# Six instead of four of eleven up-projection blocks by Strassen's method, with two more load buffers and one shared tile, in a two-layer encoder trunk on one core

## The chip, the core and the metric

The kernel runs on one core of one Trainium2 chip. The metric is device time in microseconds (us) of one execution, and lower is better. The time before is 1370.86 us, the median of three runs (1370.63 to 1371.48).

## What is computed

Two encoder layers run on 512 tokens of width 1024. Each layer has a token mixer (retention and neighbourhood attention in the first, a state-space scan in the second) and then a gated channel mixer, each between two RMS norms. The change touches the channel mixer alone, which runs once in each layer:

```python
def conv_geglu_ffn(hn, w_up, conv_w, conv_b, w_down):
    u = depthwise_conv_centered(hn @ w_up, conv_w, conv_b)   # 512x1024 @ 1024x5632
    gate, val = jnp.split(u, 2, axis=-1)                     # 2816 gate, 2816 value columns
    return (jax.nn.gelu(gate, approximate=True) * val) @ w_down
```

All data are 32-bit floats.

## The kernel before, in words

**Products of 32-bit numbers.** Each operand is kept as two tiles of the type fp32r, a high part and what is left (the names end in `h`/`hi` and `l`/`lo`). `split` makes the pair: ScalarE casts the source to the high part (`whi`, L107), and VectorE subtracts that from the source (`wlo`, L108). `mm3` multiplies with three matmuls: high by high (L116), low by high (L117) and high by low (L118). In the up projection the weights are the stationary operand and come first, so the second matmul of a product already needs the low part of its weights (the rows name them "out<-moving,stationary").

**The up projection** (`ffn`). The 2816 gate and 2816 value columns are cut into 22 tiles of 128 features, index `f`. Tiles 0 and 1 are computed together, in halves of the tokens. From then on tiles go in pairs, which makes eleven blocks with the first. A *plain* pair loads four weight units of 128x1024 (gate and value of both tiles, 512 KB each), splits each one, and makes 96 matmuls of 512 columns. A *Strassen* pair (`up_strassen`, for `f` in `UP`) treats the two tiles as a 2x2 block product over halves of the 1024 inputs and halves of the 512 tokens, with gate and value as the two rows of blocks, and needs seven block products instead of eight. Each of the seven products, `i` = 0 to 6, is 24 matmuls of 256 columns. Its weights are one of the four loaded quarters (`q[11]`, `q[12]`, `q[21]`, `q[22]`) or a sum of quarters that VectorE adds (`add`, L447), then a split of 128x1024. The combined activations come from `combos`, once in a layer. Results go from PSUM to the tiles `G` and `V` by ScalarE copies (L489) and VectorE additions (L447). The low half of `V` and the two halves of `G` each collect two products.

**Behind each tile** `tail` makes the convolution and the gate. For each of gate and value there is one ScalarE pass (L507) and two VectorE passes (L508, L509), then the activation (L514), and the product into `H` (L516).

**Buffers.** Weights of the up and down projections land in a pool of three load buffers (`wst`). A Strassen block holds three quarters there and the fourth, with one sum, in the pool `gain`. The pools `whi` and `wlo` have four buffers each. Thus the split for a product can be made when the product four before it has left TensorE. `G` and `V` alternate between two pairs of tiles.

**The down projection** (`down_strassen`) is a Strassen product too. Four of its weight combinations are built in HBM by DMAs that GpSimd issues (`sums`, L274), 32 of them in a layer. `chore(n)` starts the next n of them behind a named product of the up projection.

**Order.** The program is written in the order above, and a scheduler places the instructions on each engine's queue. Splits and weight sums stand in a section of higher priority (60). Each engine then works through its queue in that fixed order.

Of the kernel before, what the change touches and what calls it, by code (L numbers as in the profile page):

```python
# [8 lines left out]
F32 = mybir.dt.float32  # L9
R32 = mybir.dt.float32r  # L10
# [3 lines left out]
ALU = mybir.AluOpType  # L14
# [3 lines left out]
P = 128  # L18
# [7 lines left out]
HK = NF // 2  # L26
HW = S // 2
# [247 lines left out]
    return out  # L275


def down_strassen(E, big, pool, w, ts, H, first, g_post, done):

    nc, tc = E.nc, E.tc
    lower, upper = slice(0, HW), slice(HW, S)
    A11, A21 = H[:, :HK, upper], H[:, :HK, lower]
    A12, A22 = H[:, HK:, upper], H[:, HK:, lower]
    k0 = [0]

    def stage(i, u, cols):
        st = pool.tile([P, 1024], F32, name="wx", tag="k3") if k0[0] % 4 == 3 else E.wst.tile([P, 1024], F32, name="wst")
        k0[0] += 1  # L290
        nc.sync.dma_start(st[:, :cols], quarters(*i)[u])
        return st[:, :cols]

    def weights(i, u, extra=None):
        cols = 1024 if u < HK // 2 else 512
        st = stage(i, u, cols)
        if extra is None:
            hi, lo = E.whi.tile([P, 1024], R32, name="whi"), E.wlo.tile([P, 1024], R32, name="wlo")
        else:
            hi, lo = extra[:, :1024], extra[:, 1024:]  # L300
        with tc.high_priority(150):
            E.split(hi[:, :cols], lo[:, :cols], st)
        return [(hi[:, c:c + 512], lo[:, c:c + 512]) for c in range(0, cols, 512)]

    a, bb = ([E.mm.tile([P, 512], F32, name="mm") for _ in range(2)] for _ in range(2))
    d = []

    def raw(i):
        tt, stt = nc.vector.tensor_tensor, nc.vector.scalar_tensor_tensor
        if i == 1:  # L310
            s3 = big.tile([P, HK, HW], F32, name="s3")
            tt(s3, A11, A21, op=ALU.subtract)
            return s3
        if i == 2:
            tt(A21, A22, A21, op=ALU.subtract)
            stt(A11, A11, -1.0, A21, op0=ALU.mult, op1=ALU.subtract)
            return A11
        if i == 6:
            stt(A11, A12, -1.0, A11, op0=ALU.mult, op1=ALU.subtract)
            return A11  # L320
        return {3: A22, 4: A21, 5: A12}[i]

    def prepare(i):
        if i % 2:
            hi, lo = (E.res.tile([P, HK, HW], R32, name="a" + n, tag=n) for n in ("xh", "xl"))
        else:
            hi, lo = (big.tile([P, HK, HW], R32, name="a" + n, tag=n) for n in ("b1h", "b1l"))
        src = raw(i)
        for c in (slice(0, 5), slice(5, HK)):
            E.split(hi[:, c], lo[:, c], src[:, c])  # L330
        return hi, lo

    seq = ((w, 0), a), ((ts, 1), bb), ((ts, 2), a), ((ts, 3), bb), ((ts, 0), a), ((w, 2), d), ((w, 3), a)
    kept = {}
    st = {}
    op, nxt = first, None
    started = []
    for i, (src, bank) in enumerate(seq):
# [12 lines left out]
        if last:
            ex = {4: big.tile([P, 2048], R32, name="x1", tag="s3"), 5: big.tile([P, 2048], R32, name="x2", tag="e2")}
            ws = [weights(src, u, ex.get(u)) for u in range(HK // 2 + 1)]
            for t in range(2):
                for u, x in enumerate(ws):
                    if (t, u) == (0, 1):
                        E.operands()
                    if u == 1:
                        E.finish(f"t{t}", st, done)
                    mms(t, x, u)  # L360
                E.post_half(st, 2 + t, 1, bank[t], g_post, sign=-1.0)
                E.finish(f"x{2 + t} s{2 + t}", st, done)
# [24 lines left out]

UP = (6, 10, 14, 18)


def combos(E, pool, raw):


    tt, stt = E.nc.vector.tensor_tensor, E.nc.vector.scalar_tensor_tensor
    f32 = lambda ap: ap.bitcast(F32)
    lower, upper = slice(0, HW), slice(HW, S)
    out = {}
    block = lambda k, c: (slice(None), slice(4 * k, 4 * k + 4), c)

    def whole(i, k, c):  # L400
        b = block(k, c)
        tt(raw[:, i], f32(E.xh[b]), f32(E.xl[b]), op=ALU.add)
        return raw[:, i]

    def parts(n, tag, src):
        x = pool.tile([P, 2, 4, HW], R32, name="x" + n, tag=tag)
        E.split(x[:, 0], x[:, 1], src)
        out[n] = x[:, 0], x[:, 1]

    for n, k, c in (("A11", 0, upper), ("A12", 1, upper), ("A22", 1, lower)):  # L410
        out[n] = E.xh[block(k, c)], E.xl[block(k, c)]
    r1, a21 = whole(0, 1, lower), whole(1, 0, lower)
    tt(r1, r1, a21, op=ALU.subtract)
    parts("R1", "b1h", r1)
    yield out
    s2 = whole(2, 0, upper)
    tt(a21, s2, a21, op=ALU.subtract)
    parts("S3", "b1l", a21)
    yield out
    stt(s2, s2, -1.0, r1, op0=ALU.mult, op1=ALU.subtract)  # L420
    parts("S2", "s3", s2)
    yield out
    s4 = whole(3, 1, upper)
    stt(s4, s4, -1.0, s2, op0=ALU.mult, op1=ALU.subtract)
    parts("S4", "e2", s4)
    yield out


def up_strassen(E, w_up, f, X, G, V):

    nc, tc = E.nc, E.tc
    low, high = slice(0, HW), slice(HW, S)

    def load(pool, name, s, h):
        st = pool.tile([P, 1024], F32, name=name)
        nc.sync.dma_start(st.rearrange("p (f c) -> p f c", f=2),
                          w_up[s, f:f + 2, :, h * 512:h * 512 + 512].rearrange("f p c -> p f c"))
        return st  # L440
# [7 lines left out]
    q = {}  # L448

    def weights(i):  # L450
        with tc.high_priority(60):
            if i == 0:
                q[11] = load(E.wst, "wst", 0, 0)
                return parts(q[11])
            if i == 1:
                q[12], q[22] = load(E.wst, "wst", 1, 0), load(E.wst, "wst", 1, 1)
# [16 lines left out]
    for i, (n, bank) in enumerate(order):  # L473
# [15 lines left out]
                nc.scalar.copy(o, r)  # L489
        if i == 4:  # L490
            add(V[:, :, low], t, V[:, :, low])
        if i in (2, 5):
            E.chore(2)


def ffn(E, w_up, cw, w_down, ts, g_post_row, done, w1=None):
# [3 lines left out]
    with ExitStack() as ctx:  # L500
# [17 lines left out]
        def extra(tags):  # L518
# [4 lines left out]
        u0, u1, st = w1 or (E.wunit(w_up[0, 0]), E.wunit(w_up[1, 0]), None)  # L523

        behind = E.turned[1][1] if w1 else None
        w0 = [[u0, u1], [E.wunit(w_up[0, 1], extra(("b1h", "b1l")), st, behind=behind),
                         E.wunit(w_up[1, 1], extra(("e2",)), behind=behind)]]
        cwt = cp.tile([P, 2, NF, 4], F32, name="cwt")
        nc.sync.dma_start(cwt, cw)
        cwn = cp.tile([P, NF, 3], F32, name="cwn")  # L530
# [11 lines left out]
        for f in range(2, NF):  # L542
            if f in UP or f - 1 in UP:
                if f in UP:
                    G, V = (cp.tile([P, 2, S], F32, name=n, tag=t) for n, t in
                            ((("G", "k0"), ("V", "k1")) if UP.index(f) % 2 else (("G", "k2"), ("V", "k3"))))
                    up_strassen(E, w_up, f, X, G, V)
# [12 lines left out]
            if f < UP[0]:  # L560
                X = next(make)
            if f == NF - 2:
                first = [hp.tile([P, HK, HW], R32, name="a" + n, tag=n) for n in ("b1h", "b1l")]
                for k in range(0, HK, 4):
                    c = slice(k, min(k + 4, HK))
                    E.split(first[0][:, c], first[1][:, c], H[:, c, HW:])
        g_post = E.bcast(g_post_row)
        down_strassen(E, hp, cp, w_down, ts, H, first, g_post, done)


def log1p_exp_neg(E, alloc, z):
# [884 lines left out]
```

## Time and profile before

| what | us |
|---|---|
| median of three runs | 1370.86 |
| the profiled execution | 1372.97 |
| its span (first to last instruction) | 1371.2 |
| TensorE busy with matmuls | 1344.3 |
| VectorE busy | 1088.5 |
| ScalarE busy | 815.2 |
| one Strassen pair on TensorE (from `f` = 6) | 20.15 |
| one plain pair on TensorE (from `f` = 8) | 21.79 |

The profiled execution is one run, 2.11 us above the median, and 1.77 us of it lie outside its span. "PE" is TensorE, "PEld" its weight loads, "DVE" VectorE, "ACT" ScalarE, "POOL" GpSimd, and "SP" the engine that issues most DMAs. A row of the timeline gives the start, the duration, the engine and line, what is written and read, and in brackets the idle time before it and what ended that. A row of the stretches gives the stretch, its length, and the busy time of each engine in it with the number of its instructions. Instructions of VectorE overlap a little at their ends, so the distance from start to start is what one costs in an unbroken row.

### The profile page before, as it was taken

The numbers are of one execution on the slowest core, as the hardware profiler recorded it, in microseconds if no ns is written. First come the engines' busy times: TensorE is split into PE (matmuls) and PEld (weight loads), VectorE is DVE, ScalarE is ACT, GpSimd is POOL, SyncE is SP. The second block draws the span as 40 slices with busy tenths as digits, with TensorE's granted clock in tenths as the row PEclk, the third lists the DMA queues.
The fourth block names the chain that finished last, engine by engine and source line by source line (L and its number), as shares of the span: only waits on it lengthen the run. The fifth ranks groups of instructions, "written<-read, shape, count | busy, mean of one in ns | idle before, by whom it ended". The sixth has DMA issues, their size and how long they took to land.

```text
span 1371.2 us, 19491 instructions
## 1 busy us (share of the span) xinstructions
PE 1344.3 (98%) x7352; PEld 1136.2 (83%) x7352; DVE 1088.5 (79%) x1524; ACT 815.2 (59%) x1345; POOL 111.5 (8%) x130
## 2 busy tenths in 40 slices
PE   7999999999999999999999999999999999999997
PEld 6877777798999888888778788787878899998886
DVE  7368878696768889697878876898789877888876
ACT  5356667453554566664878778477555455556563
POOL 1001110100111100020000110000010001110000
PEclk9999999999999999999999999999999999999999
DMA  7443232126779946654566455174433678994654
GB/s 298 144 138 99 89 100 93 49 93 218 256 210 233 250 147 193 197 201 128 142 180 194 119 178 179 48 204 110 147 128 127 224 249 214 234 242 131 196 179 145
DMA packets 73471, 229.90 MB, mean 168 GB/s; under 512 B 8352, under 2 KB 9120, under 8 KB 72864
## 3 DMA queue, kind: packets, MB, share of 16 engines
q1 hardware_dynamic: 58320, 167.30, 37.3%
q0 software_dynamic: 7168, 46.14, 13.4%
q10 hardware_dynamic: 7888, 15.21, 4.1%
q8 instruction: 58, 0.95, 0.3%
q14 instruction: 37, 0.30, 0.1%
HBM read 221.01 MB, written 51.64 MB: 199 GB/s over the span
## 4 chain that ended last, share of the span: by engine, by line
PE 83%; ACT 6%; DVE 5%; DMA 3%; issue 2%; POOL 1%; DVEq 0%; SPq 0%; POOLq 0%; ACTq 0%
PE mm L116 23%; PE mm L118 23%; PE mm L117 23%; PE pu L118 2%; PE pu L117 2%; PE pu L116 2%; PE pi L1122 1%; PE st L1071 1%; ACT pb L1101 1%; DMA pb<-pd 1%; PE py L1142 1%; ACT whi L107 1%; DVE wlo L108 1%; DMA wst<-in_c_fm 1%; PE pt L173 1%
## 5 line engine op out<-in xcount | busy, mean ns | idle before, releaser
L116 PE MATMUL mm<-xh,whi 128*128 128x512 f32 (+1 forms) x1024 | 382.5, 374 | 0.8 <-ACT z L1041 0.4
L118 PE MATMUL mm<-xl,whi 128*128 128x512 f32 (+1 forms) x1024 | 381.6, 373 | 1.0 <-DVE xl L108 0.5
L117 PE MATMUL mm<-xh,wlo 128*128 128x512 f32 (+1 forms) x1024 | 381.3, 373 | 1.0 <-DVE wlo L108 1.0
L108 DVE TENSOR_TENSOR wlo<-wst,whi 128x1024 fp32r<-128x1024 f32 (+1 forms) x232 | 280.9, 1216 | 89.9 <-ACT whi L107 88.3
L107 ACT CAST whi<-wst 128x1024 fp32r<-128x1024 f32 (+1 forms) x232 | 239.2, 1035 | 145.8 <-PE mm L117 63.5
L116 PEld LDWEIGHTS mm<-xh,whi 128*128 128x128 f32 x1024 | 192.6, 188 | 35.9 <-issue 2.3
L118 PEld LDWEIGHTS mm<-xl,whi 128*128 128x128 f32 x1024 | 192.2, 188 | 35.6 <-issue 1.3
L117 PEld LDWEIGHTS mm<-xh,wlo 128*128 128x128 f32 x1024 | 192.6, 188 | 34.2 <-DVE wlo L108 1.4
L1101 ACT ACTIVATE pb<-pb,tok 128x128 f32<-128x128 f32 x256 | 80.8, 393 | 9.3 <-DMA pb<-pd 7.9
L507 ACT ACTIVATE cv<-mm,cwt 128x512 f32<-128x512 f32 x56 | 43.5, 777 | 68.8 <-PE mm L118 68.7
L118 PE MATMUL mm<-wlo,ab1h 128*128 128x512 f32 x164 | 64.0, 390 | 0.4 <-DVE wlo L108 0.4
L116 PE MATMUL mm<-whi,ab1h 128*128 128x512 f32 x164 | 64.0, 390 | 0.0
L117 PE MATMUL mm<-whi,ab1l 128*128 128x512 f32 x164 | 63.8, 389 | 0.0
L508 DVE SCALAR_TENSOR_TENSOR cv<-mm,cwt,cv 128x511 f32<-128x511 f32 x56 | 41.7, 745 | 22.2 <-ACT cv L507 22.2
L514 ACT ACTIVATE cv<-cv 128x512 f32<-128x512 f32 x44 | 27.8, 632 | 42.8 <-DVE cv L509 42.8
L1035 DVE SCALAR_TENSOR_TENSOR xf<-mm,cwt,xf 128x511 f32<-128x511 f32 (+1 forms) x64 | 47.6, 745 | 6.2 <-ACT xf L1032 5.8
L274 POOL DMA_DIRECT2D ts<-in_f_down x48 | 30.0, 668 | 261.7 <-PE mm L118 227.7
L509 DVE SCALAR_TENSOR_TENSOR cv<-mm,cwt,cv 128x511 f32<-128x511 f32 x56 | 41.8, 746 | 0.9
L116 PE MATMUL mm<-whi,yh 128*128 128x512 f32 x104 | 40.8, 394 | 1.5 <-DVE xf L1035 1.5
L1154 POOL TENSOR_TENSOR sq<-sq 128x512 f32<-128x512 f32 x11 | 16.7, 1516 | 309.1 <-ACT sq L1148 244.6
L117 PE MATMUL mm<-whi,yl 128*128 128x512 f32 x104 | 41.1, 395 | 0.0
L116 PE MATMUL mm<-whi,xh 128*128 128x512 f32 x104 | 40.7, 398 | 0.0
(359 smaller groups left out, 2919.7 us busy)
## 6 DMA issues: line engine op xcount, KB each, us to landing
wst<-in_f_up SPq DMA_DIRECT2D x80, 512.0 KB
ts<-in_f_down POOLq DMA_DIRECT2D x48, 704.0 KB, 6.2
wst<-in_c_fm SPq DMA_DIRECT2D x40, 512.0 KB
wst<-ts SPq DMA_DIRECT2D x32, 512.0 KB
pb<-pd ACTq DMA_DIRECT2D x29, 512.0 KB
wst<-in_f_down SPq DMA_DIRECT2D x24, 512.0 KB
ts<-ts POOLq DMA_DIRECT2D x16, 704.0 KB, 9.9
wst<-in_ab_fm SPq DMA_DIRECT2D x20, 512.0 KB
```

Source lines behind the costliest of these rows:

```text
L107: first = self.nc.scalar.copy(hi, src)
L108: second = self.nc.vector.tensor_tensor(lo, src, hi.bitcast(F32), op=ALU.subtract)
L116: mm(out, lh, rh, start=first, stop=False)
L117: mm(out, ll, rh, start=False, stop=False)
L118: self.product = mm(out, lh, rl, start=False, stop=last)
L274: out.append(lambda i=i, src=src, j=j, c=c, kw=kw: gp.dma_start(part(ts, i, c), part(src, j, c), **kw))
L507: nc.scalar.activation(o, ps, AF.Identity, scale=w(1), bias=w(3))
L508: nc.vector.scalar_tensor_tensor(o[:, 1:], ps[:, :S - 1], w(0), o[:, 1:], op0=ALU.mult, op1=ALU.add)
L509: nc.vector.scalar_tensor_tensor(o[:, :S - 1], ps[:, 1:], w(2), o[:, :S - 1], op0=ALU.mult, op1=ALU.add)
L514: nc.scalar.activation(g, g, AF.Gelu_apprx_tanh)
L1035: nc.vector.scalar_tensor_tensor(r[:, a], ps[:, b], wc(j), r[:, a], op0=ALU.mult, op1=ALU.add)
L1101: nc.scalar.activation(pb[:, dr, c], pb[:, dr, c], AF.Identity, scale=1.0 - 2 * dr, bias=tok[:, 0, c, dr * H + h:dr * H + h + 1])
```

## The change

1. `UP` becomes (6, 8, 10, 14, 16, 18). The pairs at 8 and 16 are now Strassen pairs, in both layers. Before, each Strassen pair stood between plain pairs; now there are two groups of three in a row.
2. The first quarter of a Strassen block, `q[11]`, is loaded into a buffer of its own (name `wu`), alternating between two tiles `e0` and `e1`, and no longer into `wst`.
3. The four split combined activations share one tile, `xc`, instead of four tags. It has the tag `big`, which the operands of the down projection take over afterwards (`big[:, 0]`, `big[:, 1]`, and `big[:, 2]` for weights).
4. The first operand that the down projection prepares, a difference, is made in three pieces through `e0` and `e1` instead of one piece in a tile of its own.
5. A Strassen block starts one chore behind each of the products 1, 3 and 5, instead of two behind 2 and 5.

```diff
-        if i == 1:
-            s3 = big.tile([P, HK, HW], F32, name="s3")
-            tt(s3, A11, A21, op=ALU.subtract)
-            return s3
...
-            hi, lo = (big.tile([P, HK, HW], R32, name="a" + n, tag=n) for n in ("b1h", "b1l"))
+            hi, lo = big[:, 0], big[:, 1]
+        if i == 1:
+            for n, c in enumerate((slice(0, 4), slice(4, 8), slice(8, HK))):
+                s3 = hp.tile([P, 4, HW], F32, name="s3", tag=f"e{n % 2}")[:, :c.stop - c.start]
+                nc.vector.tensor_tensor(s3, A11[:, c], A21[:, c], op=ALU.subtract)
+                E.split(hi[:, c], lo[:, c], s3)
+            return hi, lo
...
-UP = (6, 10, 14, 18)
+UP = (6, 8, 10, 14, 16, 18)
...
-    def parts(n, tag, src):
-        x = pool.tile([P, 2, 4, HW], R32, name="x" + n, tag=tag)
-        E.split(x[:, 0], x[:, 1], src)
-        out[n] = x[:, 0], x[:, 1]
+    x = pool.tile([P, 4, 2, 4, HW], R32, name="xc", tag="big")
+
+    def parts(n, i, src):
+        E.split(x[:, i, 0], x[:, i, 1], src)
+        out[n] = x[:, i, 0], x[:, i, 1]
...
-                q[11] = load(E.wst, "wst", 0, 0)
+                q[11] = load(pool, "wu", 0, 0, f"e{UP.index(f) % 2}")
...
-        if i in (2, 5):
-            E.chore(2)
+        if i in (1, 3, 5):
+            E.chore()
...
-                first = [hp.tile([P, HK, HW], R32, name="a" + n, tag=n) for n in ("b1h", "b1l")]
+                big = hp.tile([P, 3, HK, HW], R32, name="big")
                 for k in range(0, HK, 4):
                     c = slice(k, min(k + 4, HK))
-                    E.split(first[0][:, c], first[1][:, c], H[:, c, HW:])
+                    E.split(big[:, 0, c], big[:, 1, c], H[:, c, HW:])
```

In the changed kernel every line of `up_strassen`, `ffn` and what follows stands four lines further down (L447 becomes L451, L489 L493, L507 to L516 L511 to L520); `split` and `mm3` keep their lines.

**VectorE's queue behind the last split of a Strassen block.** Before, at the block of `f` = 10, in the first layer. The first row is the split for product 6. The `wlo<-wst` rows after it are units of the plain pair that follows, L447 are additions into `G` and `V`, and L508 begins the tail.

```order
L108 TENSOR_TENSOR wlo<-wst,whi 128x1024
L447 TENSOR_TENSOR G<-pu,G 128x256 x2
L108 TENSOR_TENSOR wlo<-wst,whi 128x1024
L447 TENSOR_TENSOR V<-w_3745,V 128x2x256
L108 TENSOR_TENSOR wlo<-wst,whi 128x1024
L447 TENSOR_TENSOR G<-pu,G 128x256 x2
L108 TENSOR_TENSOR wlo<-wst,whi 128x1024
L508 SCALAR_TENSOR_TENSOR cv_3811<-G,cwt,cv_3811 128x511
```

Now, at the block of `f` = 6, which another Strassen block follows. The first row is again the split for product 6. The row `wlo<-wu` is the split for product 0 of the next block, and the L451 rows of 128x1024 are its weight sums.

```order
L108 TENSOR_TENSOR wlo<-wst,whi 128x1024
L451 TENSOR_TENSOR G<-pu,G 128x256 x2
L108 TENSOR_TENSOR wlo<-wu,whi 128x1024
L451 TENSOR_TENSOR wu<-wu,wst 128x1024
L451 TENSOR_TENSOR V<-w_3337,V 128x2x256
L451 TENSOR_TENSOR wst<-wst 128x1024
L451 TENSOR_TENSOR G<-pu,G 128x256
L451 TENSOR_TENSOR gain<-wu,wst 128x1024
L451 TENSOR_TENSOR G<-pu,G 128x256
L108 TENSOR_TENSOR wlo<-wst,whi 128x1024
L512 SCALAR_TENSOR_TENSOR cv_3402<-G,cwt,cv_3402 128x511
L108 TENSOR_TENSOR wlo<-gain,whi 128x1024
```

The three weight sums of the next block have moved between the additions into `G` and `V`, ahead of the tail. The same queue goes on with the tail of the first block up to the split for product 3 of the second (the last row here; the row `gain<-gain` is the sum that it reads):

```order
L513 SCALAR_TENSOR_TENSOR cv_3402<-G,cwt,cv_3402 128x511
L512 SCALAR_TENSOR_TENSOR cv_3407<-V,cwn,cv_3407 128x511
L512 SCALAR_TENSOR_TENSOR cv_3412<-G,cwt,cv_3412 128x511
L513 SCALAR_TENSOR_TENSOR cv_3407<-V,cwn,cv_3407 128x511
L513 SCALAR_TENSOR_TENSOR cv_3412<-G,cwt,cv_3412 128x511
L520 TENSOR_TENSOR H<-cv_3402,cv_3407 128x512
L512 SCALAR_TENSOR_TENSOR cv_3417<-V,cwn,cv_3417 128x511
L451 TENSOR_TENSOR gain<-gain 128x1024
L513 SCALAR_TENSOR_TENSOR cv_3417<-V,cwn,cv_3417 128x511
L520 TENSOR_TENSOR H<-cv_3412,cv_3417 128x512
L108 TENSOR_TENSOR wlo<-gain,whi 128x1024
```

The whole tail of one Strassen block now stands ahead of product 3's split of the next.

**VectorE's queue where the down projection's difference is made.** Before, inside the last Strassen block (`f` = 18), in one piece:

```order
L108 TENSOR_TENSOR wlo<-gain,whi 128x1024
L312 TENSOR_TENSOR s_4833<-H 128x2816
L108 TENSOR_TENSOR wlo<-wst,whi 128x1024
```

Now the first piece stands in the block of `f` = 16, behind the split for product 0 of the block of `f` = 18 (`wlo<-wu`), a second piece one block later, and the third in the down projection:

```order
L451 TENSOR_TENSOR G<-pu,G 128x256 x2
L108 TENSOR_TENSOR wlo<-wu,whi 128x1024
L327 TENSOR_TENSOR s_5047<-H 128x1024
L451 TENSOR_TENSOR V<-w_4509,V 128x2x256
L451 TENSOR_TENSOR wu<-wu,wst 128x1024
```

The first piece has moved ahead of the last Strassen block's weight sums. GpSimd's queue has the same rows as before, and the second layer's channel mixer has the same order as the first's.

More of the change, by code (lines that the diff above doesn't have):

```diff
@@ L275, in sums, with down_strassen @@
     return out
-def down_strassen(E, big, pool, w, ts, H, first, g_post, done):
+def down_strassen(E, hp, pool, w, ts, H, big, g_post, done):
     nc, tc = E.nc, E.tc
@@ L299, in weights @@
         else:
-            hi, lo = extra[:, :1024], extra[:, 1024:]
+            hi, lo = extra
         with tc.high_priority(150):
@@ L335, in down_strassen @@
     st = {}
-    op, nxt = first, None
+    op, nxt = (big[:, 0], big[:, 1]), None
     started = []
@@ L351, in down_strassen @@
         if last:
-            ex = {4: big.tile([P, 2048], R32, name="x1", tag="s3"), 5: big.tile([P, 2048], R32, name="x2", tag="e2")}
+            x = big[:, 2].rearrange("p k c -> p (k c)")
+            ex = {4: (x[:, :1024], x[:, 1024:2048]), 5: [hp.tile([P, 1024], R32, name="x2", tag=n) for n in ("e0", "e1")]}
             ws = [weights(src, u, ex.get(u)) for u in range(HK // 2 + 1)]
@@ L413, in combos @@
     tt(r1, r1, a21, op=ALU.subtract)
-    parts("R1", "b1h", r1)
+    parts("R1", 0, r1)
     yield out
@@ L417, in combos @@
     tt(a21, s2, a21, op=ALU.subtract)
-    parts("S3", "b1l", a21)
+    parts("S3", 1, a21)
     yield out
     stt(s2, s2, -1.0, r1, op0=ALU.mult, op1=ALU.subtract)
-    parts("S2", "s3", s2)
+    parts("S2", 2, s2)
     yield out
@@ L424, in combos, with up_strassen, load @@
     stt(s4, s4, -1.0, s2, op0=ALU.mult, op1=ALU.subtract)
-    parts("S4", "e2", s4)
+    parts("S4", 3, s4)
     yield out
-def up_strassen(E, w_up, f, X, G, V):
+def up_strassen(E, pool, w_up, f, X, G, V):
     nc, tc = E.nc, E.tc
     low, high = slice(0, HW), slice(HW, S)
-    def load(pool, name, s, h):
-        st = pool.tile([P, 1024], F32, name=name)
+    def load(pool, name, s, h, tag=None):
+        st = pool.tile([P, 1024], F32, name=name, tag=tag or name)
         nc.sync.dma_start(st.rearrange("p (f c) -> p f c", f=2),
@@ L525, in ffn @@
         behind = E.turned[1][1] if w1 else None
-        w0 = [[u0, u1], [E.wunit(w_up[0, 1], extra(("b1h", "b1l")), st, behind=behind),
-                         E.wunit(w_up[1, 1], extra(("e2",)), behind=behind)]]
+        w0 = [[u0, u1], [E.wunit(w_up[0, 1], extra(("big",)), st, behind=behind),
+                         E.wunit(w_up[1, 1], extra(("e0", "e1")), behind=behind)]]
         cwt = cp.tile([P, 2, NF, 4], F32, name="cwt")
@@ L546, in ffn @@
                             ((("G", "k0"), ("V", "k1")) if UP.index(f) % 2 else (("G", "k2"), ("V", "k3"))))
-                    up_strassen(E, w_up, f, X, G, V)
+                    up_strassen(E, hp, w_up, f, X, G, V)
                     for j in range(2):
@@ L562, in ffn @@
             if f == NF - 2:
-                first = [hp.tile([P, HK, HW], R32, name="a" + n, tag=n) for n in ("b1h", "b1l")]
+                big = hp.tile([P, 3, HK, HW], R32, name="big")
                 for k in range(0, HK, 4):
                     c = slice(k, min(k + 4, HK))
-                    E.split(first[0][:, c], first[1][:, c], H[:, c, HW:])
+                    E.split(big[:, 0, c], big[:, 1, c], H[:, c, HW:])
         g_post = E.bcast(g_post_row)
-        down_strassen(E, hp, cp, w_down, ts, H, first, g_post, done)
+        down_strassen(E, hp, cp, w_down, ts, H, big, g_post, done)
 def log1p_exp_neg(E, alloc, z):
```

## The prediction

> **What bounds the kernel now.** I read the page's totals and its chain first, then stretches of the first layer's up projection, then the timelines of TensorE and VectorE in them.
>
> ```profile
> PE 1344.3 (98%) x7352; PEld 1136.2 (83%) x7352; DVE 1088.5 (79%) x1524; ACT 815.2 (59%) x1345; POOL 111.5 (8%) x130
> ...
> PE 83%; ACT 6%; DVE 5%; DMA 3%; issue 2%; POOL 1%; DVEq 0%; SPq 0%; POOLq 0%; ACTq 0%
> ...
> L118 PE MATMUL mm<-wlo,ab1h 128*128 128x512 f32 x164 | 64.0, 390 | 0.4 <-DVE wlo L108 0.4
> ```
>
> TensorE is 98% busy and carries 83% of the chain that ended last. So fewer matmul columns pay directly, as long as nothing else comes late. In the down projection (last row) TensorE idled 0.4 us in all. The pairs `f` = 6 to 19, Strassen and plain in turn:
>
> ```profile
> core 0: us, PE busy (x) PEld busy (x) DVE busy (x) ACT busy (x) POOL busy (x), PEclk, DMA share, GB/s
> 342.70:362.85 20.15, 20.15 (x169) 20.14 (x168) 12.75 (x16) 11.75 (x19) 2.91 (x6) 1.00 0.69 243
> 362.85:384.64 21.79, 21.79 (x98) 18.03 (x97) 20.58 (x25) 10.87 (x15) 0.97 (x2) 1.00 0.64 235
> 384.64:404.79 20.15, 20.15 (x169) 20.14 (x168) 11.50 (x14) 9.54 (x16) 3.68 (x5) 1.00 0.77 206
> 404.79:426.58 21.79, 21.79 (x98) 18.04 (x97) 20.66 (x26) 12.85 (x18) 2.61 (x3) 1.00 1.05 264
> ...
> sum 145.97, PE 145.97 PEld 134.67 DVE 116.17 ACT 81.53 POOL 18.85; mean PE 20.85 PEld 19.24 DVE 16.60 ACT 11.65 POOL 2.69
> ```
>
> TensorE has no gap at all here. VectorE is busy only 12 to 13 us in a Strassen pair but over 20 in the plain pair behind it: it does the Strassen pair's tail and the next one's weight sums in the plain pair. That is the cover which the change takes away. That the ends of the stretches are the pairs' ends shows in TensorE's timeline (columns of a matmul change from 512 to 256 and back):
>
> ```profile
> 342.48 0.39 PE L118 MATMUL mm<-xl,whi 128*128 128x512 f32 x1
> 342.70 0.28 PE L116 MATMUL mm<-xh,whi 128*128 128x256 f32 x1
> 342.81 0.28 PE L117 MATMUL mm<-xh,wlo 128*128 128x256 f32 x1
> ...
> 362.73 0.28 PE L118 MATMUL mm<-xS,whi 128*128 128x256 f32 x1
> 362.85 0.40 PE L116 MATMUL mm<-xh,whi 128*128 128x512 f32 x1
> ...
> 384.64 0.28 PE L116 MATMUL mm<-xh,whi 128*128 128x256 f32 x1
> ```
>
> **Matmuls: the gain.** A Strassen pair is 168 matmuls in 20.15 us, 0.120 us each and 2.88 us a product; a plain pair is 96 in 21.79, 0.227 each. Half the columns cost more than half the time, so a pair that turns from plain to Strassen saves 1.64 us and not an eighth of 21.79 (2.72). Two pairs in two layers: 4 x 1.64 = 6.6 us. The second layer's pairs are the same:
>
> ```profile
> 1091.67:1111.82 20.15, 20.15 (x170) 20.15 (x168) 13.11 (x16) 12.09 (x19) 2.91 (x6) 1.00 0.71 242
> ```
>
> [...]
>
> **VectorE: the loss.** The prices, as distances from start to start in unbroken rows of its timeline:
>
> ```profile
> 352.89 1.23 DVE L108 TENSOR_TENSOR wlo<-wst,whi 128x1024 fp32r<-128x1024 f32 x1 [1.66 <-ACT whi L107]
> 354.03 0.81 DVE L447 TENSOR_TENSOR G<-pu,G 128x256 f32<-128x256 f32 x2
> 355.49 1.23 DVE L108 TENSOR_TENSOR wlo<-wst,whi 128x1024 fp32r<-128x1024 f32 x1 [0.65 <-ACT whi L107]
> 357.70 0.69 DVE L447 TENSOR_TENSOR V<-w,V 128x512 f32<-128x512 f32 x1 [0.98 <-ACT w L489]
> ...
> 361.60 1.23 DVE L108 TENSOR_TENSOR wlo<-wst,whi 128x1024 fp32r<-128x1024 f32 x1 [1.00 <-ACT whi L107]
> 362.75 0.75 DVE L508 SCALAR_TENSOR_TENSOR cv<-G,cwt,cv 128x511 f32<-128x511 f32 x1
> 363.43 0.75 DVE L508 SCALAR_TENSOR_TENSOR cv<-V,cwn,cv 128x511 f32<-128x511 f32 x1
> 364.10 0.74 DVE L509 SCALAR_TENSOR_TENSOR cv<-G,cwt,cv 128x511 f32<-128x511 f32 x1
> ...
> 366.08 0.68 DVE L516 TENSOR_TENSOR H<-cv,cv 128x512 f32<-128x512 f32 x1
> 366.69 0.74 DVE L509 SCALAR_TENSOR_TENSOR cv<-G,cwt,cv 128x511 f32<-128x511 f32 x1
> ...
> 420.21 1.21 DVE L447 TENSOR_TENSOR gain<-wst 128x1024 f32<-128x1024 f32 x1
> 421.35 0.74 DVE L509 SCALAR_TENSOR_TENSOR cv<-mm,cwt,cv 128x511 f32<-128x511 f32 x1
> ...
> 425.18 1.21 DVE L108 TENSOR_TENSOR wlo<-gain,whi 128x1024 fp32r<-128x1024 f32 x1
> 426.43 1.22 DVE L447 TENSOR_TENSOR gain<-gain 128x1024 f32<-128x1024 f32 x1
> ```
>
> So a split costs 1.14 (352.89 to 354.03), a weight sum 1.14 (420.21 to 421.35), a pass of a convolution 0.66 (363.43 to 364.10 and on), a product into `H` 0.61, an addition into `G` 0.39 (half of 0.81, less the overlap), into `V` 0.61 (0.69 less the overlap of 0.08 that the other rows show). Where an instruction needs what the one ahead does, it waits some 0.1 more (425.18 to 426.43 is 1.25).
>
> One Strassen pair asks for 7 splits (7.98), 4 weight sums (4.56), 4 additions into `G` (1.56), one into `V` (0.61), 8 passes (5.28) and 2 products into `H` (1.22): 21.2, with about 0.3 for three such waits 21.5 us. TensorE takes 20.15. A lone Strassen pair spreads this over 41.9 us with its plain neighbour. Three in a row can't.
>
> How far behind it gets follows from the queues shown with the change. Call the pairs of a group A, B, C, and count from A's start on TensorE. A starts as before, with VectorE waiting for free weight buffers. Behind A's last split stands B's first, and it can't start before the `whi` buffer of A's product 3 is free. In the trace the same place is the row at 355.49, 12.79 after 342.70; the cast ahead of it waited for TensorE:
>
> ```profile
> 354.41 1.05 ACT L107 CAST whi<-wst 128x1024 fp32r<-128x1024 f32 x1 [1.56 <-PE pu L118]
> ```
>
> From 12.79 on there is no more such wait, and up to B's split for product 3 there stand three splits (3.42), four weight sums (4.56), the addition into `V` (0.61), two into `G` (0.78), eight passes (5.28), two products into `H` (1.22) and three short waits (0.3): 16.2. That split starts at 29.0 and ends 1.22 later, at 30.2. TensorE reaches product 3 of B at 20.15 + 3 x 2.88 = 28.8 and needs the low part for its second matmul at 28.9. It stalls **1.3 us**.
>
> From there to C's split for product 3, one full pair's work stands in the queue, 21.5 us against TensorE's 20.15: another **1.3**. In the second group the first piece of the down projection's difference (128x1024, 1.14 as a sum of that size) stands in this stretch too, so there it is 2.5. Behind C come plain pairs, where four splits (4.56), eight passes and two products into `H` (6.5) fill 11.1 of 21.79 us, and the backlog goes.
>
> A group loses 2.6, the second one 3.8: 6.4 in a layer, **12.8** in both. What bounds this term: from below nothing, if VectorE kept up; from above the case of full durations below.
>
> **The rest, at nothing.** The loads are as many and as large as before (four quarters for four units), and `wu` lets the first be issued a block ahead. Three chores in a Strassen pair instead of four, and two at the end, leave the same DMAs; they are needed from the down projection's second product on, and the last four only in its fourth. ScalarE gains 3 casts and 10 small copies in a new Strassen pair, against at most 13 of 20 us in the stretches above. The shared tile frees later than single tags did, but its next writer stands behind the pair `f` = 20. In the down projection the difference costs one more split and one more sum in part; TensorE's 0.4 us idle there say that such work is covered.
>
> **Sum.** 1371.2 (span) - 6.6 + 12.8 = 1377.4; against the median, 2.1 us under the profiled execution, 1370.86 + 6.2 = **1377.1**.
>
> **The rivals.**
>
> 1. *VectorE keeps up* (faster). If TensorE never waits, the time is 1370.86 - 6.6 = 1364.3. It decides where the stalls are under 6.6 us: VectorE's rows would have to be some 4% shorter: B then loses 0.6, C 0.5 and the extra piece 1.1, 2 x (2 x 1.1 + 1.1) = 6.6. For it: on average it has room, since 116.17 plus two times 10.1 (three splits, four sums, the additions) is 136 of 143 us. Against: the order is fixed, and the room lies in A and behind C.
> 2. *Half of the loss* (same). If B's split comes in time, since the run starts earlier than 12.79, and only C lags, 2 x (1.3 + 2.5) = 7.6 are lost, and the time is 1371.9.
> 3. *Late loads* (slower still). The additions in HBM crowd the loads:
>
> ```profile
> 404.70 1.05 ACT L107 CAST whi<-wst 128x1024 fp32r<-128x1024 f32 x1 [4.13 <-DMA wst<-in_f_up]
> ```
>
> Such a wait cost nothing in a plain pair. In B or C each one adds in full: four of them, one in a group, 16.5 us and 1393; at a quarter of that, 1381. Against it stand the earlier `wu` and the fewer chores.
> 4. *Full durations.* If each VectorE instruction began only when the one ahead had ended, the stretch before B's product 3 would be 17.4 and a full pair 23.1 before the short waits: B loses 2.5, C 3.2 and 4.4, 25 in all, 1389. The row at 363.43 starts 0.07 before the one at 362.75 ends, which speaks against it. [...]
>
> **Chances.** My forecast 0.70, rival 1 0.12, rival 2 0.12, rival 3 0.04, rival 4 0.02. About 0.2%, 2.7 us, is what a measurement of this kernel can tell from no change. Faster by more 0.12, within it 0.13 (rival 2 and a little of the forecast), slower 0.75. The forecast's own range is 1373.6 to 1381, 12.8 give or take 3.6 for waits that I counted at 0.1. From 1370.2 to 1382.5 it takes in most of rival 2 and the mild end of rival 3.
>
> **What would show it.** TensorE should wait for `wlo` (L108) in the pairs at 8, 10, 16 and 18, some 1.3 us each (2.5 at 18), first at product 3; the pair at 6 should still take 20.15. VectorE should be busy nearly all of the stretches of the pairs 8 and 10. The pairs 6 to 19 should take 142.7 + 6.4 = 149 us instead of 145.97. I am wrong if TensorE shows no waits there, if the waits are for a load, or if the down projection has new gaps.

## The result, and the profile after

The changed kernel takes 1377.76 us (median of 7 runs, 1376.57 to 1380.70) against 1371.78 for the kernel before on the same chip: ratio 1.0044, 95% interval 1.0030 to 1.0058. It is slower, by 6.0 us; the prediction said 6.2. The times below come from several chips, so each experiment is compared by its ratio to runs of the kernel before on its own chip; differences between two experiments are differences of these ratios, 0.1% being 1.4 us.

The page of the changed kernel, totals and the chain by engine:

```profile
PE 1342.7 (97%) x7640; PEld 1145.7 (83%) x7640; DVE 1125.3 (82%) x1578; ACT 838.5 (61%) x1399; POOL 108.3 (8%) x130
...
PE 77%; DVE 12%; ACT 4%; DMA 4%; issue 2%; POOL 1%; SPq 1%; DVEq 0%; POOLq 0%; ACTq 0%
```

VectorE's share of the chain has gone from 5 to 12%, and TensorE's from 83 to 77: the path now runs through VectorE at some places. The first layer's pairs from 6 to 19, now three Strassen pairs, a plain one and three Strassen pairs, show at which:

```profile
core 0: us, PE busy (x) PEld busy (x) DVE busy (x) ACT busy (x) POOL busy (x), PEclk, DMA share, GB/s
342.77:362.93 20.16, 20.16 (x170) 20.16 (x169) 14.97 (x18) 11.53 (x19) 2.44 (x5) 1.00 0.74 258
362.93:384.25 21.32, 20.41 (x170) 20.21 (x169) 21.02 (x27) 14.17 (x24) 1.46 (x3) 1.00 0.58 196
384.25:405.71 21.46, 20.95 (x171) 20.37 (x170) 17.96 (x23) 13.01 (x21) 1.92 (x3) 1.00 0.55 185
405.71:427.49 21.78, 21.78 (x99) 18.01 (x98) 21.46 (x26) 12.14 (x18) 1.78 (x2) 1.00 0.85 199
427.49:447.65 20.16, 20.16 (x170) 20.16 (x169) 15.26 (x19) 11.53 (x19) 4.33 (x5) 1.00 0.97 218
447.65:468.98 21.33, 20.42 (x171) 20.22 (x170) 20.98 (x27) 13.19 (x23) 2.60 (x3) 1.00 0.82 190
468.98:491.50 22.52, 21.17 (x170) 20.36 (x169) 20.70 (x26) 13.90 (x24) 2.60 (x3) 1.00 0.87 221
sum 148.73, PE 145.05 PEld 139.48 DVE 132.35 ACT 89.47 POOL 17.13; mean PE 20.72 PEld 19.93 DVE 18.91 ACT 12.78 POOL 2.45
```

The first pair of each group takes the bare 20.16. The pairs 8, 10, 16 and 18 take 1.2, 1.3, 1.2 and 2.4 us more: 6.0 in the layer. The whole is 148.73 instead of 145.97 before. The second layer's gaps add up to the same 6.0, so the two layers lose 5.5 us, nearly all of the 6.0 between the medians. (The two profiled executions, 1380.18 and 1372.97, both lie above their medians and are 7.2 apart; the rest of that is outside these stretches.)

What TensorE waits for in pair 8, from the timeline of the changed kernel (TensorE, its third and fourth row from the pair at 18, then VectorE from pair 6's product 4 on):

```profile
371.56 0.40 PE L116 MATMUL pu<-xh,whi 128*128 128x256 f32 x2
372.87 0.39 PE L117 MATMUL pu<-xh,wlo 128*128 128x256 f32 x1 [0.91 <-DVE wlo L108]
...
475.86 0.39 PE L117 MATMUL mm<-xc,wlo 128*128 128x256 f32 x1 [0.75 <-DVE wlo L108]
...
479.80 0.38 PE L116 MATMUL mm<-xc,whi 128*128 128x256 f32 x1 [0.44 <-ACT whi L107]
...
355.56 1.23 DVE L108 TENSOR_TENSOR wlo<-wu,whi 128x1024 fp32r<-128x1024 f32 x1 [0.65 <-ACT whi L107]
...
368.35 0.74 DVE L512 SCALAR_TENSOR_TENSOR cv<-V,cwn,cv 128x511 f32<-128x511 f32 x1
369.01 1.21 DVE L451 TENSOR_TENSOR gain<-gain 128x1024 f32<-128x1024 f32 x1
370.15 0.74 DVE L513 SCALAR_TENSOR_TENSOR cv<-V,cwn,cv 128x511 f32<-128x511 f32 x1
370.99 0.69 DVE L520 TENSOR_TENSOR H<-cv,cv 128x512 f32<-128x512 f32 x1
371.60 1.22 DVE L108 TENSOR_TENSOR wlo<-gain,whi 128x1024 fp32r<-128x1024 f32 x1
372.73 1.22 DVE L108 TENSOR_TENSOR wlo<-wu,whi 128x1024 fp32r<-128x1024 f32 x1
```

Product 3 begins at 371.56, and its second matmul needs the low part whose split runs from 371.60 to 372.82. VectorE has no pause from 355.56 to there. Between stand the weight sums, but also the whole convolution tail of pair 6 (lines L512, L513, L520), for which TensorE does not wait in pair 8. In the pairs at 10 and 18 a part of the gap is a wait for ScalarE, 0.44 us in each (the row at 479.80): the cast of product 4's weights stands on its queue behind the cast of product 3's sum, which VectorE makes late.

### The profile page after: what moved, and what is told of

Read it like the earlier page. It is cut to its first block, busy times and chain, and to the rows that moved or that the text cites. A ratio compares the mean times of both kernels' runs of the same rounds, so it can differ in the third digit from the quotient of the medians.

```text
span 1378.4 us, 20207 instructions
## 1 busy us (share of the span) xinstructions
PE 1342.7 (97%) x7640; PEld 1145.7 (83%) x7640; DVE 1125.3 (82%) x1578; ACT 838.5 (61%) x1399; POOL 108.3 (8%) x130
## 4 chain that ended last, share of the span: by engine, by line
PE 77%; DVE 12%; ACT 4%; DMA 4%; issue 2%; POOL 1%; SPq 1%; DVEq 0%; POOLq 0%; ACTq 0%
PE mm L116 20%; PE mm L118 20%; PE mm L117 20%; DVE wlo L108 3%; PE pu L117 2%; PE pu L118 2%; PE pu L116 2%; DVE cv L512 1%; PE pi L1126 1%; PE st L1075 1%; DVE gain L451 1%; DMA pb<-pd 1%; DVE cv L513 1%; PE py L1146 1%; DMA wst<-in_c_fm 1%
## 5 line engine op out<-in xcount | busy, mean ns | idle before, releaser
L116 PE MATMUL mm<-xh,whi 128*128 128x512 f32 (+2 forms) x928 | 341.7, 368 | 0.6 <-ACT xh L107 0.2
L117 PE MATMUL mm<-xh,wlo 128*128 128x512 f32 (+2 forms) x928 | 340.6, 367 | 1.2 <-DVE wlo L108 1.2
L118 PE MATMUL mm<-xl,whi 128*128 128x512 f32 (+2 forms) x928 | 340.7, 368 | 0.5 <-DVE xl L108 0.5
L116 PEld LDWEIGHTS mm<-xh,whi 128*128 128x128 f32 (+1 forms) x928 | 174.7, 188 | 30.8 <-issue 2.5
L117 PEld LDWEIGHTS mm<-xh,wlo 128*128 128x128 f32 (+1 forms) x928 | 174.7, 188 | 29.4 <-DVE wlo L108 1.6
L118 PEld LDWEIGHTS mm<-xl,whi 128*128 128x128 f32 (+1 forms) x928 | 174.4, 188 | 29.8 <-issue 1.3
L116 PE MATMUL mm<-xc,whi 128*128 128x256 f32 x288 | 81.6, 284 | 1.8 <-ACT whi L107 1.8
L117 PE MATMUL mm<-xc,wlo 128*128 128x256 f32 x288 | 81.7, 284 | 1.5 <-DVE wlo L108 1.5
L118 PE MATMUL mm<-xc,whi 128*128 128x256 f32 x288 | 81.4, 283 | 0.0
L116 PE MATMUL mm<-whi,big 128*128 128x512 f32 x164 | 64.0, 390 | 0.0
L117 PE MATMUL mm<-whi,big 128*128 128x512 f32 x164 | 63.8, 389 | 0.0
L511 ACT ACTIVATE cv<-mm,cwt 128x512 f32<-128x512 f32 x40 | 31.0, 776 | 53.0 <-PE mm L118 53.0
L116 PEld LDWEIGHTS mm<-xc,whi 128*128 128x128 f32 x288 | 55.1, 192 | 2.6 <-ACT whi L107 2.6
L118 PEld LDWEIGHTS mm<-xc,whi 128*128 128x128 f32 x288 | 55.3, 192 | 0.0
```

The lines of the kernel that those rows point to most:

```text
L116: mm(out, lh, rh, start=first, stop=False)
L117: mm(out, ll, rh, start=False, stop=False)
L118: self.product = mm(out, lh, rl, start=False, stop=last)
L511: nc.scalar.activation(o, ps, AF.Identity, scale=w(1), bias=w(3))
```

## The experiments

In the stretch from the pair at 6 to the end of the pair at 18, six Strassen pairs and a plain one without any stall take 6 x 20.16 + 21.78 = 142.74. Where a kernel has three in a row, that is the number to compare with.

**1. Everything but the two new pairs.**

```diff
-UP = (6, 8, 10, 14, 16, 18)
+UP = (6, 10, 14, 18)
```

> The changed kernel with UP = (6, 10, 14, 18) again: the new load buffers, the shared tile, the difference in three pieces and one chore behind products 1, 3, 5 stay, but each Strassen pair has a plain neighbour. If VectorE's work in three Strassen pairs in a row is the cause, the whole difference goes: no TensorE wait in the pairs 6 to 19 (145.97 us for them), and the time is that of the kernel before within 1 us, ratio 1.000. If the new buffers, the shared tile or the chores cost something themselves, it stays above the kernel before by 2 us or more.

Measured: 1371.40 us, ratio 0.9992 (0.9983 to 1.0000). The pairs 6 to 19 take 145.98 again. The extra buffers, the shared tile, the pieces and the other chores together cost nothing that can be measured; if anything they save 0.08%. So what the change loses is in the two new pairs.

**2. VectorE's order, with its work unchanged.** Two kernels give the section with the loads, weight sums and splits of a Strassen pair another priority. The loads and ScalarE's casts move with it; but in the changed kernel VectorE had no pause ahead of the late split, so an earlier load or cast alone could not have helped there.

```diff
-        with tc.high_priority(60):
+        with tc.high_priority(100):
```

> The changed kernel with the weights of a Strassen pair placed further ahead (priority 100 instead of 60 in that section), nothing else: the same instructions, but on VectorE's queue the fourth weight sum and the split for product 3 of the next pair now stand ahead of nearly the whole tail. Theory 'place in the queue': the tail can wait, and its backlog is worked off in the plain pairs behind the group, so TensorE has no wait in the pairs 6 to 19 (142.7 us for them), and the time is the kernel before less 6.6, ratio 0.995. Theory 'amount of work': a Strassen pair asks VectorE for 21.5 us where TensorE takes 20.15, so three in a row lag in any order; waits of 1 to 1.5 us a pair remain in the pairs 10 and 18 at least, 1368 to 1377. Theory 'late loads': nothing changes, ratio 1.0044.

```diff
-        with tc.high_priority(60):
+        with tc.high_priority(40):
```

> The other way: the weights of a Strassen pair placed less far ahead (priority 40 instead of 60), nothing else. 'Place in the queue': more of the tail stands ahead of the splits, and TensorE waits longer in each of the two groups, 8 to 9 us in a layer instead of 6; 1382 to 1384, ratio 1.009. 'Amount of work' and 'late loads': the same work and the same loads, so the time of the changed kernel, ratio 1.0044.

At 40: 1386.69 us, ratio 1.0105 (1.0088 to 1.0122). It is slower, as the first theory said, and by more: the stretch takes 152.66, so 9.9 us are lost in a layer where 8 to 9 were expected:

```profile
341.96:494.62 152.66, 147.49 (x1105) 141.21 (x1104) 133.67 (x162) 89.37 (x141) 17.11 (x24) 0.99 0.74 202
```

At 100 the time is 1377.79 us, ratio 1.0045 (1.0025 to 1.0064), as if nothing had changed, which is what the theory of late loads gave. But inside, two things have. The first group has no stall at all: 60.47 us for three pairs, 62.94 in the changed kernel, with the same 54 us of VectorE in both. The second group gives most of it back:

```profile
343.08:403.55 60.47, 60.47 (x505) 60.47 (x504) 54.06 (x67) 39.50 (x64) 5.80 (x11) 1.00 0.65 215
...
445.49:471.22 25.73, 21.91 (x170) 21.71 (x169) 20.19 (x27) 13.90 (x24) 2.60 (x3) 0.93 0.67 153
```

The timeline at priority 100: VectorE at the place shown above, then SP, VectorE, ScalarE and TensorE in the pair at 16:

```profile
364.08 1.22 DVE L451 TENSOR_TENSOR gain<-gain 128x1024 f32<-128x1024 f32 x1
365.22 0.75 DVE L512 SCALAR_TENSOR_TENSOR cv<-G,cwt,cv 128x511 f32<-128x511 f32 x1
...
367.20 1.22 DVE L108 TENSOR_TENSOR wlo<-gain,whi 128x1024 fp32r<-128x1024 f32 x1
...
436.92 0.53 SPq L442 DMA_DIRECT2D gain<-in_f_up  x1
...
451.04 1.23 DVE L451 TENSOR_TENSOR gain<-gain 128x1024 f32<-128x1024 f32 x1 [4.61 <-DMA gain<-in_f_up]
...
452.30 1.04 ACT L107 CAST whi<-gain 128x1024 fp32r<-128x1024 f32 x1 [4.28 <-DVE gain L451]
...
454.82 0.63 ACT L493 COPY G<-mm 128x256 f32<-128x256 f32 x2
...
451.13 0.28 PE L118 MATMUL pu<-xc,whi 128*128 128x256 f32 x1
455.23 0.39 PE L116 MATMUL mm<-xc,whi 128*128 128x256 f32 x1 [3.82 <-ACT G L493]
...
457.25 0.41 PE L117 MATMUL mm<-xc,wlo 128*128 128x256 f32 x1
...
459.38 0.41 PE L118 MATMUL mm<-xc,whi 128*128 128x256 f32 x1
```

In pair 8 the sum for product 3 now stands ahead of the tail, and its split starts 4.0 us after the pair's start (367.20 - 363.23), instead of 8.7 (371.60 - 362.93). In the pair at 16 the same sum is at the head of VectorE's queue at 446.4, but the load that it adds, issued at 436.92, comes 14 us later. (In the changed kernel that load is issued at 439.34 and its sum runs at 453.73 without a wait, since the tail stands ahead of it.) ScalarE's queue has the cast of that sum ahead of the copy that empties product 0's bank, so the copy waits too, and TensorE stands still for 4.0 us (451.25 to 455.23) for a bank that could have been free long before. VectorE stands still once more at the end of the group, for a cast that waits for a load, and the down projection behind it loses 3.9 us by the distances from start to start (the last row is of another view, the waits by engine, and counts 3.2 of it as idle):

```profile
495.62 1.05 ACT L107 CAST whi<-wst 128x1024 fp32r<-128x1024 f32 x1 [6.77 <-DMA wst<-in_f_up]
...
496.71 1.23 DVE L108 TENSOR_TENSOR wlo<-wst,whi 128x1024 fp32r<-128x1024 f32 x1 [6.58 <-ACT whi L107]
```

```profile
PE mm L118 <- DVE wlo L108: 3.2, 2, 2.6
```

The second layer had little of this in that execution (0.6 us in the pairs, 1.8 in the down projection), and runs spread from 1373.35 to 1386.50. So the expected order came about and the expected time did not: the new waits begin with loads.

**3. Whether loads are what takes it.** Two kernels leave out the sixteen additions in HBM of each layer, so that four weight combinations of the down projection stay unsummed; one stands at each priority. Two more move the chores.

```diff
 # at priority 100
-                out.append(lambda i=i, src=src, j=j, c=c, kw=kw: ...)
+                if not op: out.append(lambda i=i, src=src, j=j, c=c, kw=kw: ...)
```

> The kernel with priority 100, without the sixteen additions in HBM that each layer issues from GpSimd (so the second layer of weights for the down projection's summed products stays unsummed; the copies stay). Theory: at priority 100 VectorE's queue is in a good order, and what takes the gain away is that loads crowded by those additions land late (14 us for one in the pair at 14). Then both up projections run without stalls but for a few tenths, 142.7 us from the pair at 6 to the pair at 18's end, the gaps in the down projection go too, and the time is some 11 us under that of priority 100: about 1366 us, ratio 0.996 or less. Rival: it is the order itself (tails put off, casts ahead of copies) that holds TensorE up; then the stall of 5.5 us and the down projection's gaps stay, and the time stays near 1377, ratio 1.004.

```diff
 # the same line out, at priority 60
```

> The changed kernel (priority 60), also without the sixteen additions in HBM. Theory: its stalls are VectorE's order alone and no load is late, so the stalls for the low parts of weights stay as they are, 6.0 us a layer, pairs 6 to 18 at 148.7 us; the time is 1375 to 1378, ratio 1.003 to 1.005. Rival (late loads are behind VectorE's lateness): the stalls go, 1366 us, ratio 0.996.

Without the additions, priority 100 takes 1365.52 us, ratio 0.9955 (0.9940 to 0.9969), and the stretch is 142.74, the bare number. At priority 60 it takes 1382.46, ratio 1.0073 (1.0059 to 1.0087), and the stalls stay, so late loads are no part of the changed kernel's loss. These two kernels differ in the priority alone, and on one chip they are 16.9 us apart: with no load in the way, that is what the order is worth. The time at priority 60 is 4.5 us above what I had expected. The first group and pair 16 lose the same as in the changed kernel. In pair 18 VectorE's rows stand in another order with the additions gone, TensorE's waits there follow closely on one another (2.3 us lost from 478.37 to 481.02), and behind them the granted clock is 0.50 for 3.37 us (third row; more on this at the end). That makes the stretch 1.5 us longer, in the second layer too, and twice that is most of the 4 us by which the two ratios differ.

```profile
341.69:484.43 142.74, 142.74 (x1106) 138.97 (x1105) 129.00 (x160) 90.09 (x144) 4.86 (x10) 1.00 0.48 156
```

```profile
343.54:493.76 150.22, 146.28 (x1106) 140.92 (x1104) 133.83 (x163) 91.30 (x145) 4.86 (x10) 0.99 0.46 150
...
481.02:484.39 3.37, 3.37 (x16) 3.37 (x16) 3.37 (x4) 1.55 (x3) 0.00 (x0) 0.50 0.71 246
```

(The first row is priority 100 without additions, the other two priority 60 without.) Then all additions kept, but issued elsewhere, at priority 100:

```diff
-        if i in (1, 3, 5):
+        if i in ((1, 3, 5) if f < 12 else (5,)):
             E.chore()
...
-            E.chore(2)
+            E.chore(3)
```

> Priority 100 with all additions kept but issued elsewhere: three chores instead of two behind a plain block, and one instead of three in each of the pairs at 14, 16 and 18. If late loads are all that stands against priority 100, and no other loads come late from the denser copies at the start, the time is about 1366 us, ratio 0.996, faster than both kernels. If the additions only move their crowding to another stage, the loss comes back in the pairs 8 and 10 or the plain pair at 12: 1370 to 1378.

```diff
-        if i in (1, 3, 5):
+        if i in (1, 3, 5) and f < 12:
             E.chore()
...
-            E.chore(2)
+            E.chore(4 if f < 6 else 3)
```

> Priority 100, six Strassen blocks, all additions kept: four chores behind each of the first four plain blocks, three behind each plain block after that, three in the pairs at 6, 8 and 10, and none in 14, 16 and 18. If additions beside the loads of the pairs 14 to 18 are what made the version with one chore in each of these pairs swing between 1366 and 1380, this one is steady at about 1366 (ratio 0.996). If the denser chores ahead make loads late elsewhere (the plain blocks 2 to 5, or the pair at 14 behind the plain pair with six chores), 1370 or more, with waits for loads at those places.

The first swings from run to run: 1365.66 to 1380.17 in 12 runs, median 1372.95, ratio 1.0005 (0.9986 to 1.0023). Its profiled execution is the fastest of them, and there the stretch has no stall; what holds the slower runs up is not shown:

```profile
341.79:484.52 142.73, 142.73 (x1105) 138.96 (x1104) 129.20 (x160) 90.12 (x145) 15.60 (x21) 1.00 0.77 206
```

The second is bad in every run: 1384.41 us, ratio 1.0094 (1.0078 to 1.0111). Its load for pair 8 now comes late, behind the denser chores ahead:

```profile
369.44 1.23 DVE L451 TENSOR_TENSOR gain<-gain 128x1024 f32<-128x1024 f32 x1 [6.48 <-DMA gain<-in_f_up]
```

So moving the chores this way moved the crowding. With the additions in either place, six blocks at priority 100 did not hold the time that they have without them.

**4. Less work for VectorE, in the old order.** The products into `H` of the Strassen pairs go to GpSimd, at priority 60.

```diff
-            nc.vector.tensor_tensor(H[:, f], g, v, op=ALU.mult)
+            (nc.gpsimd if neg else nc.vector).tensor_tensor(H[:, f], g, v, op=ALU.mult)
```

> The changed kernel (priority 60) with the two products into H of each Strassen pair on GpSimd instead of VectorE (1.22 us of VectorE less in a pair). By the prediction's working (the amount of VectorE's work in a run decides) B's stall falls from 1.3 to 0.1, C's from 1.3 to 0.1 and in the second group to 1.2: 1.5 us a layer are left of 6.0, and the time falls by 9 to about 1369, ratio 0.998. If the order of the queue decides more than the amount, half of the stalls or more stay (3 us a layer): 1372, ratio 1.000. If GpSimd's products hold up VectorE's, no gain: 1377 or more.

Measured: 1387.46 us, ratio 1.0118 (1.0101 to 1.0134), 10 us behind the changed kernel; the third theory it was. GpSimd and VectorE at pair 8, from the timeline:

```profile
366.45 3.44 POOL L520 TENSOR_TENSOR H<-cv,cv 128x512 f32<-128x512 f32 x1 [6.36 <-DVE cv L513]
...
370.59 2.13 POOL L520 TENSOR_TENSOR H<-cv,cv 128x512 f32<-128x512 f32 x1 [0.21 <-DVE cv L513]
...
366.85 0.74 DVE L512 SCALAR_TENSOR_TENSOR cv<-V,cwn,cv 128x511 f32<-128x511 f32 x1
367.51 1.22 DVE L451 TENSOR_TENSOR gain<-gain 128x1024 f32<-128x1024 f32 x1
368.65 1.78 DVE L513 SCALAR_TENSOR_TENSOR cv<-V,cwn,cv 128x511 f32<-128x511 f32 x1
...
371.49 2.31 DVE L108 TENSOR_TENSOR wlo<-wu,whi 128x1024 fp32r<-128x1024 f32 x1
```

A pass that takes 0.74 alone took 1.78 beside one GpSimd product, and a split of 1.22 took 2.31: each of the two products (0.61 on VectorE) cost VectorE some 1.05 elsewhere. The rows don't show it for GpSimd's whole span: inside the 3.44 us from 366.45 a pass (366.85) and a weight sum (367.51) kept their 0.74 and 1.22. Why a VectorE row grows there is not shown. The experiment therefore tells nothing on the amount of VectorE's work, since it took none away.

**5. The load buffer.** `q[11]` is loaded into `wst` again, at priority 60.

```diff
-                q[11] = load(pool, "wu", 0, 0, f"e{UP.index(f) % 2}")
+                q[11] = load(E.wst, "wst", 0, 0)
```

> The changed kernel with the first quarter of a Strassen pair loaded into the common load buffers again, not into the two new ones. If the waits are VectorE's, the loads have slack and the time stays that of the changed kernel within 1.5 us, with the same eight waits for the low parts. If the loads are near the edge, three buffers for four quarters make them late: TensorE then waits for casts or sums that wait for a load, and the time is 1380 or more.

Measured: 1397.87 us, ratio 1.0184 (1.0165 to 1.0203), 19 us behind the changed kernel, where I expected the same. The stretch is 7.8 us longer (its row first), and VectorE's queue waits for a load in it (a row of the timeline):

```profile
343.30:499.84 156.54, 148.54 (x1105) 142.27 (x1104) 131.16 (x159) 88.49 (x140) 17.11 (x24) 0.98 0.75 202
```

```profile
384.00 1.23 DVE L451 TENSOR_TENSOR wst<-wst 128x1024 f32<-128x1024 f32 x1 [1.45 <-DMA wst<-in_f_up]
```

With `q[11]` in it, `wst` holds three quarters of the running pair, and the next pair's second quarter isn't loaded ahead. VectorE has two such waits in the stretch, 5.0 us in all. How much of the 7.8 is due to them and how much to the somewhat different order that came with it, I did not separate.

**6. One group of three, with cover in the second.** The pair at 16 is plain again, at each priority; and four blocks at priority 100.

```diff
-UP = (6, 8, 10, 14, 16, 18)
+UP = (6, 8, 10, 14, 18)
 # and high_priority(100)
```

> Priority 100 with five Strassen blocks, 16 plain again (6, 8, 10, 14, 18). Theory: the first group of three had no stall at priority 100, and with a plain pair between 14 and 18 the late load of the pair at 16 has cover. From the kernel with four such blocks (1371.4) one pair in each layer saves 2 x 1.64 = 3.3: 1368 us, ratio 0.997. Rival (three in a row ask too much of VectorE whatever its order): a group of three loses 2.4 in each layer, 1373, ratio 1.001.

```diff
 # the same five at high_priority(60)
```

> Priority 60 with five Strassen blocks (6, 8, 10, 14, 18): one group of three and no second. By the terms as measured so far: from the kernel with four (1371.4) one pair in a layer saves 1.64, and the group of three loses 1.2 in the pair at 8 and 1.2 in the pair at 10, so a layer is 0.8 longer: 1372.9 us, ratio 1.000 to 1.002, and 6 us behind the same five blocks at priority 100 (2 x 2.4 of it in stalls). Rival (priority 100 is faster for another reason, outside the group): no waits for low parts in 8 and 10 here, or a time near 1368.

```diff
-UP = (6, 8, 10, 14, 16, 18)
+UP = (6, 10, 14, 18)
 # and high_priority(100)
```

> Priority 100 with four Strassen blocks and a plain pair behind each. Theory: priority 100 has nothing to mend where no three stand in a row, so the time is that of four blocks at priority 60, 1371.4, ratio 0.999, give or take 0.15%. Rival: priority 100 is faster by itself: 1368, ratio 0.997. The other rival: tails put off cost something in the plain pairs: 1374, ratio 1.001.

| blocks | priority 60 | priority 100 |
|---|---|---|
| four | 0.9992 (0.9983 to 1.0000) | 0.9996 (0.9986 to 1.0006) |
| five, 16 plain | 0.9992 (0.9982 to 1.0003) | 0.9962 (0.9949 to 0.9976) |
| six (60: the changed kernel) | 1.0044 (1.0030 to 1.0058) | 1.0045 (1.0025 to 1.0064) |

Five blocks at priority 100 take 1366.76 us: 0.38% faster than the kernel before, and some 11 us faster than the changed one. It is the fastest version that computes everything and holds its time (1366.08 to 1369.35). Its first group takes the bare 60.48 (first row), where at priority 60 it takes 62.93 (second row, the other kernel):

```profile
342.69:403.17 60.48, 60.48 (x506) 60.47 (x505) 54.03 (x67) 39.24 (x64) 5.80 (x11) 1.00 0.67 214
```

```profile
341.71:404.64 62.93, 61.50 (x505) 60.71 (x504) 53.98 (x66) 37.83 (x61) 5.80 (x11) 1.00 0.64 212
```

That is 2.45 in a layer, 4.9 in both; the two times differ by 0.30%, 4.1. (Five blocks at priority 60 came out slightly better than the 1.000 to 1.002 expected.) Priority 100 alone brings nothing where no three stand in a row (four blocks).

## Why the prediction was right, and where it was not

- **Matmuls: the gain, 6.6 us.** Held. A Strassen pair without stalls is 20.16, and the stretch without any is 142.74 (142.7 said).
- **VectorE: the loss, 1.3 + 1.3 and 1.3 + 2.5 in a layer, 6.4.** Measured 1.2, 1.3, 1.2, 2.4: 6.0. The count of the queue was close: from 355.56 to the split for product 3 at 371.60 it is 16.0 us, 16.2 said; the run began 12.79 after the pair's start, as before. From there to the split for product 3 of pair 10, at 393.17, it is 21.6, 21.5 said. The pair at 18 has the extra piece of the difference, as said. Its first wait comes at product 2 already (the row at 475.86), where I had said product 3, and in the pairs at 10 and 18 part of the wait is for a cast, where I had said splits alone. I had also said that VectorE would be busy nearly all of the pairs at 8 and 10. It was in the pair at 8 (21.02 of 21.32 us) but not in the pair at 10 (17.96 of 21.46).
- **"The rest, at nothing."** Held as a sum (experiment 1), and the down projection has no new gaps. But without the buffer `wu` the kernel takes 19 us more (experiment 5). The prediction called it a help and gave it no price.
- **The sum, 6.2 us.** Measured 6.0, with an interval of 1.9 us to either side. That the two are 0.2 apart is partly luck; that the terms are right shows in the stretches.
- **"A lone Strassen pair spreads this. Three in a row can't."** Wrong, though the number came out right. The kernel at priority 100 has the same VectorE work, and its group of three ran without a stall, VectorE busy for 54 of 60.5 us. The 21.5 us that a pair asks need not all be done within 20.15, since tails can go behind the group. What cost 6.0 us in a layer was the order: tails standing ahead of the sum and the split for product 3. My step counted everything in the queue ahead of that split, which is right for the given order, and then gave the amount of work as the reason.
- **Rival 1 (VectorE keeps up, 1364.3).** It did not here. The time that the rival gave was about that of six blocks without stalls (1365.52, additions left out).
- **Rival 2 (B's split in time).** No: the pair at 8 lost 1.2, about as much as the pair at 10.
- **Rival 3 (late loads).** Not in the changed kernel: without the additions its stalls stayed. But late loads are what holds six blocks at priority 100 back, and there they cost more than the whole gain (ratio 1.0045 with the additions, 0.9955 without).
- **Rival 4 (full durations).** Out: the splits at 371.60 and 372.73 stand 1.13 apart and last 1.22 each.
- **Two readings that enter no forecast.** VectorE's busy time in the two Strassen pairs shown is 11.5 and 12.75 us, not "12 to 13", and rival 3's sum comes to 1393.6.

## What to carry to other kernels

When an engine's queue is late at one instruction, ask first what stands ahead of it that nobody waits for; a sum over its work tells capacity, and a queue can miss a date with capacity to spare. Bringing dated work forward also brings forward its waits for loads, and in an in-order queue such a wait holds up everything behind it, on the next engine too (in experiment 2 VectorE waited 4.61 us for a load, ScalarE 4.28 behind it and TensorE 3.82). What paid here was to bring the dated work forward and to take the pair whose load is late out of the run (five blocks instead of six). And price a long stall above its length (a wait of 4.0 us cost 5.6, below).

## What the runs showed of the hardware

A TensorE that stood still for 4.0 us came back slower. The granted clock (PEclk, the number behind POOL's in each row) at priority 100, before that wait, just after it, and behind that:

```profile
448.37:451.25 2.88, 2.88 (x26) 2.84 (x24) 0.21 (x1) 0.00 (x0) 0.00 (x0) 1.00 0.88 255
455.23:457.50 2.27, 2.27 (x15) 2.27 (x16) 2.27 (x5) 1.94 (x5) 0.00 (x0) 0.76 1.04 208
457.50:459.60 2.10, 2.10 (x12) 2.10 (x11) 2.10 (x3) 0.78 (x2) 0.00 (x0) 0.50 0.04 8
459.60:462.48 2.88, 2.88 (x25) 2.88 (x25) 2.88 (x5) 1.32 (x2) 0.00 (x0) 0.96 0.00 0
```

For about a microsecond matmuls ran at full pace, then at half the clock: from 457.25 to 459.38, ten of them, 0.213 us each instead of 0.120. The pair at 16 lost 25.73 - 20.15 = 5.6 us to a wait of 4.0. The waits of about 1 us in the changed kernel left the clock at 1.00 (its stretches above).

Shorter stops than 4.0 us were enough elsewhere. In the kernel with the chores early, TensorE stood still for 2.2 us in the pair at 16 (458.56 to 460.77) and then had half the clock for 3.41 us:

```profile
460.77 0.38 PE L116 MATMUL mm<-xc,whi 128*128 128x256 f32 x1 [2.06 <-ACT G L493]
```

```profile
461.47:464.88 3.41, 3.41 (x18) 3.41 (x17) 3.41 (x6) 2.02 (x4) 0.00 (x0) 0.50 0.02 5
```

At priority 60 without additions, three waits of 1.1, 0.7 and 0.4 us close together did the same (its third row above). In each of these three cases the spell at half the clock lasted 3.2 to 3.4 us and cost about 1.5 us more than the waits themselves (by the paces above: 3.3 us at 0.213 us a matmul hold what takes 1.9 us at 0.120). It can last longer: in the pair at 8 of the kernel with the chores early, behind a wait of 5.7 us that ended at 373.63, the clock was 0.50 for at least 5.3 us:

```profile
373.63:376.00 2.37, 2.37 (x11) 2.37 (x12) 2.37 (x5) 1.72 (x4) 0.00 (x0) 0.50 0.18 35
376.00:378.92 2.92, 2.92 (x16) 2.92 (x15) 2.92 (x5) 0.91 (x2) 0.00 (x0) 0.50 0.00 0
```

How long a stop must be to bring the lower clock, and what ends it, these runs do not show.
